# An encoder block on one core: the weights' sums of the feed-forward part spread over four stages

## The chip, the cores and the metric

The kernel runs on 1 core of one Trainium2 chip. The metric is the device time of one execution, in microseconds (us). The engines are TensorE (PE; its weight loads are PEld), VectorE (DVE), ScalarE (ACT), GpSimd (POOL) and SyncE (SP). Every DMA of this kernel is issued by SP, in one order; a DMA that has to wait for something holds up all that stand behind it on SP. A compile-time scheduler lays down the order of instructions on each engine; where the code calls `tc.keep_in_program_order`, the instructions so marked stay in the order of the code.

## The reference

One layer of a bidirectional encoder for two sequences of 512 tokens of width 1024, all in float32:

```python
mod = silu(c) @ w_ada + b_ada              # sh1, sc1, gt1, sh2, sc2, gt2
h = rmsnorm(x, g_attn) * (1 + sc1) + sh1
qa, ka, va, cq, ckv, kr, gla, glb = split(h @ w_in)
oa = windowed attention of qa, ka, va      # 8 heads, 2 key/value heads, +-128 tokens, sink
ob = dense attention from cq, ckv, kr      # 8 heads, low-rank q and kv
mix = sigmoid(gla) * (oa @ w_o_a) + sigmoid(glb) * (ob @ w_o_b)
x = x + gt1 * (mix @ w_out)
h2 = rmsnorm(x, g_ffn) * (1 + sc2) + sh2
u = dwconv3(h2 @ w_up)                     # to 2 x 2816 columns
x = x + gt2 * ((silu(ug) * ua) @ w_down)   # ua, ug: the two halves of u
```

## The kernel before

Matrix products are made of three matmuls each: a float32 operand is split into a high part (`hi`) and what is left (`lo`), and hi x hi, hi x lo and lo x hi are added (`mm3`, L80 to L82). The split of a weight is an operation of two halves: by POOL (`split_pool`, L70 and L73) or by ACT and DVE (`split_fast`, L76 and L77).

The program runs in stages. Up to about 230 us: modulation, norms, the projections of the attentions. From there to about 600 us: the two attentions. To about 693 us: the output weights of both mixers and the gates (`branches`), which leave `m_hi`, `m_lo`. To about 800 us: the product with `w_out` and the second norm (`project_half`). To about 1190 us: the first product of the feed-forward part and the convolution. The rest is the product with `w_down`.

**The weights' sums.** The first feed-forward product goes, for each of its 22 column chunks of 2 x 128, with seven block products instead of eight (Strassen's scheme in Winograd's form). For that, four sums of the four blocks of the chunk's weights are needed. They are made ahead, in the attention stage, by the generator `weight_sums` (L504 to L529), and are kept in DRAM, in `su_d`, which is read only in the feed-forward stage (`wraw<-su_d`, L764 by way of L969). The generator handles 44 half chunks. For each it loads a tile `wsum` of 128 x 4 x 256 (512 KB, L514), makes four sums on POOL in place (L522, L523, L525, L526), and stores the tile to `su_d` (L528). There are two buffers `wsum`. Loads, sums and stores are all pinned to the order of the code. Of each half, the load of the next half is put ahead of the sums, and the store behind them:

```python
for n, (c, cs) in enumerate(halves):
    t = ts[n]
    load(n + 1)
    pin(G.tensor_add(t[:, 3], t[:, 2], t[:, 3]))
```

A half takes three steps of the generator; the attention's loop advances it once a turn (`next(wsum, None)` at its end), and what is left is run through after the loop. The loop has 128 units of attention, 8 dense blocks (`PairB`) of 8 and 4 windowed blocks (`GroupA`) of 16.

**What stands around it.** Each turn of the loop also gives five matmuls of the generator `gates` (`psg`, L495) to PE, which fills the time between attention units. Every 24 of them end in a copy `go` by ACT (L499, two buffers) and a store of it (L500). The softmax (L531 to L540) scales its tile `p` on POOL (L539); PE then transposes `p` into `ppt` (L545). So POOL's sums and the `p` that PE waits for share one queue. The inputs of the windowed blocks are loaded as `lda` (L637), the outputs are stored as `o` (L614, L711), and the gates' weights are `wg_raw` (L480) and `wg`.

**Behind it.** In the branches the attention's output comes back as `o_raw` (2 MB each), and per pair of output chunks four tiles `wo_raw` (L804) are loaded and split by POOL into `wo`; PE's products are `psy`, 24 matmuls for each output chunk and sequence, 96 for a pair. `gt` is the load of the gates (L810). Behind the third pair of four the first half of `w_out` is loaded and split by POOL (`w_half(0)`, tiles `wraw` with seven buffers and `wt` with eight). `project_half(0)` makes the first 512 columns of the eight token tiles (`psx`, 24 matmuls each, over k = 0 to 7), adds x and stores (`x_d<-x`, L885; `x1_d` in the code). `w_half(1)` brings the second half of `w_out` (8 raw tiles, L762 to L764, split by ACT and DVE), and `project_half(1)` makes the other columns, the norm and the operands of the feed-forward part. There `tmp` gives small tiles; its kind `tmp_cc` (128 x 512) has six buffers.

## Time and profile before

| what | value |
|---|---|
| median of three runs | 1458.52 us (1457.64 to 1461.35) |
| the profiled execution | 1463.69 us |
| its span in the trace | 1461.9 us |
| PE busy | 1395.4 us, 95% of the span |
| PEld, weight loads beside PE | 1155.7 us, 79% |
| DVE, ACT, POOL busy | 64%, 46%, 42% |
| the chain that ended last | PE 78%, DVE 10%, DMA 5%, POOL 3%, ACT 2% |

The profile is of one execution. Its busy shares are means over stages with different limits, so the stretches have to be looked at one by one; the 5% of DMA and 3% of POOL in the chain lie where PE stood still for them. The granted clock of PE is a share of the higher of two levels (2.4 and 1.2 GHz).

### The profile page before, as it was taken

The page shows a single profiled execution, that of the slowest core. Times are in us where ns is not written, and L with a number is a line of the kernel's source. Part 1 is how long each engine was busy: PE and PEld are TensorE (multiplying, and loading weights), DVE is VectorE, ACT ScalarE, POOL GpSimd, SP SyncE. Part 2 cuts the span into 40 slices and gives each one's busy share as a digit, 9 for nine tenths or more (in the row PEclk, how much of TensorE's full clock was granted, in tenths as well). Part 3 has the DMA queues.
Part 4 walks back from the last instruction along what each step waited for, and adds up shares of the span by engine and source line. Part 5 has one row for each costly group of instructions (what it writes and reads, how often), then busy time and mean ns, then how long its engine had stood idle before and what let it go on. Part 6 is the DMA issues. An engine that isn't in the chain of part 4 may idle for free.

```text
span 1461.9 us, 21179 instructions
## 1 busy us (share of the span) xinstructions
PE 1395.4 (95%) x7184; PEld 1155.7 (79%) x7184; DVE 941.7 (64%) x1885; ACT 679.5 (46%) x1385; POOL 609.0 (42%) x702
## 2 busy tenths in 40 slices
PE   5888997999999899999998999999999999999998
PEld 4777776888878787787887888888888887888887
DVE  4788774666668786564369776666666668347433
ACT  3475223666666566332136765555555554212210
POOL 3175023676677787455003232222222235444430
PEclk9999999999999999999999999999999999999999
DMA  8565764666666667855432344444434447646522
GB/s 320 195 209 178 239 234 159 196 227 202 227 198 220 208 212 250 286 174 177 143 115 80 108 130 130 125 127 123 130 123 127 132 122 250 205 140 222 185 80 72
DMA packets 162620, 255.19 MB, mean 175 GB/s; under 512 B 21192, under 2 KB 86984, under 8 KB 159440
## 3 DMA queue, kind: packets, MB, share of 16 engines
q1 hardware_dynamic: 162512, 253.84, 53.2%
q8 instruction: 57, 0.93, 0.3%
q14 instruction: 51, 0.42, 0.1%
HBM read 186.67 MB, written 67.13 MB: 174 GB/s over the span
## 4 chain that ended last, share of the span: by engine, by line
PE 78%; DVE 10%; DMA 5%; POOL 3%; ACT 2%; issue 2%; SPq 0%; ACTq 0%; POOLq 0%; DVEq 0%
PE px L980 15%; PE psg L495 9%; PE py L980 8%; PE psd L80 5%; PE psd L81 5%; PE psd L82 5%; PE pz L980 4%; PE ppt L545 3%; PE ppo L608 2%; PE psx L82 2%; PE psx L81 2%; PE psx L80 2%; PE psz L80 1%; PE psz L82 1%; PE psz L81 1%
## 5 line engine op out<-in xcount | busy, mean ns | idle before, releaser
L959 POOL TENSOR_TENSOR wt<-wraw,wt 128x512 fp32r<-128x512 f32 x88 | 119.4, 1363 | 395.4 <-ACT wt L958 362.9
L980 PE MATMUL px<-t,wt 128*128 128x512 f32 x792 | 190.0, 389 | 1.7 <-ACT tmp_cc L985 1.7
L980 PEld LDWEIGHTS px<-t,wt 128*128 128x128 f32 x792 | 148.5, 188 | 33.1 <-ACT tmp_cc L985 2.4
L495 PE MATMUL psg<-h_hi,wg 128*128 128x512 f32 x512 | 172.1, 401 | 0.0
L77 DVE TENSOR_TENSOR wd<-wraw,wd 128x512 fp32r<-128x512 f32 x88 | 96.3, 1133 | 90.8 <-ACT wd L76 90.8
L80 PE MATMUL psd<-wd 128*128 128x512 f32 x352 | 137.0, 389 | 0.1
L82 PE MATMUL psd<-wd 128*128 128x512 f32 x352 | 136.9, 389 | 0.0
L81 PE MATMUL psd<-wd 128*128 128x512 f32 x352 | 136.9, 389 | 0.0
L76 ACT CAST wd<-wraw 128x512 fp32r<-128x512 f32 x88 | 50.8, 619 | 151.5 <-issue 112.7
L958 ACT CAST wt<-wraw 128x512 fp32r<-128x512 f32 x154 | 93.9, 619 | 39.7 <-POOL wt L959 26.5
L495 PEld LDWEIGHTS psg<-h_hi,wg 128*128 128x128 f32 x512 | 97.0, 192 | 18.7 <-POOL wg L73 0.8
L539 POOL TENSOR_SCALAR p<-p,l 128x512 f32<-128x512 f32 (+2 forms) x128 | 78.3, 615 | 63.7 <-DVE l L538 45.9
L495 PE MATMUL psg<-h_lo,wg 128*128 128x512 f32 x256 | 102.7, 401 | 0.0
L537 ACT ACTIVATE p<-pps,nm 128x512 f32<-128x512 f32 (+2 forms) x128 | 78.1, 610 | 39.2 <-DVE nm L534 31.3
L992 DVE SCALAR_TENSOR_TENSOR tmp_u<-tmp_cc,cw,tmp_u 128x511 f32<-128x511 f32 x66 | 57.2, 867 | 41.5 <-ACT tmp_u L991 41.4
L70 POOL TENSOR_SCALAR wd<-wraw 128x512 fp32r<-128x512 f32 x44 | 33.6, 764 | 112.5 <-PE psd L82 84.9
L80 PEld LDWEIGHTS psd<-wd 128*128 128x128 f32 x352 | 66.1, 188 | 14.3 <-issue 0.5
L82 PEld LDWEIGHTS psd<-wd 128*128 128x128 f32 x352 | 66.1, 188 | 13.8
L81 PEld LDWEIGHTS psd<-wd 128*128 128x128 f32 x352 | 66.1, 188 | 13.5
L534 DVE TENSOR_REDUCE nm<-pps 128x1 f32<-128x512 f32 (+2 forms) x128 | 74.7, 584 | 3.2 <-PE pps L82 1.5
L545 PE MATMUL ppt<-ident,p 128*128 128x128 f32 x416 | 66.9, 274 | 8.2 <-POOL p L539 8.2
L73 POOL TENSOR_TENSOR wd<-wraw,wd 128x512 fp32r<-128x512 f32 x44 | 73.1, 1661 | 3.7
(256 smaller groups left out, 3425.7 us busy)
## 6 DMA issues: line engine op xcount, KB each, us to landing
w_ada<-in_w_ada_dram SPq DMA_DIRECT2D x24, 1024.0 KB, 5.5
wsum<-in_w_up_dram SPq DMA_DIRECT2D x44, 512.0 KB, 3.9
su_d<-wsum SPq DMA_DIRECT2D x44, 512.0 KB, 3.6
wraw<-su_d SPq DMA_DIRECT2D x88, 256.0 KB, 3.1
wraw<-in_w_down_dram SPq DMA_DIRECT2D x88, 256.0 KB, 3.2
wraw<-in_w_up_dram SPq DMA_DIRECT2D x66, 256.0 KB, 2.7
g_d<-tmp_u SPq DMA_DIRECT2D x44, 256.0 KB, 2.4
wraw<-g_d SPq DMA_DIRECT2D x44, 256.0 KB, 3.5
```

The costliest lines, as they stand in the source:

```text
L77: V.tensor_sub(lo, raw, hi.bitcast(F32))
L80: PE.matmul(ps, lhsT=lh, rhs=rh, start=first, stop=False)
L81: PE.matmul(ps, lhsT=lh, rhs=rl, start=False, stop=False)
L82: PE.matmul(ps, lhsT=ll, rhs=rh, start=False, stop=last)
L495: PE.matmul(ps, lhsT=ws[n][:, wl, k, :], rhs=hl[b][:, k, :], start=k == 0 and i == 0, stop=k == KD - 1 and i == 2)
L534: V.tensor_reduce(nm, ps[:, :n], op=ALU.max, axis=AX.X, negate=True)
L537: A.activation(p[:, :n], ps[:, :n], AF.Exp, bias=nm, accum_out=l)
L539: G.tensor_scalar(out=p[:, :plen], in0=p[:, :plen], scalar1=l, scalar2=1.0, op0=ALU.mult, op1=ALU.mult)
L545: PE.transpose(pt[:, j * 128:(j + 1) * 128], p[:, j * 128:(j + 1) * 128], ident)
L958: A.copy(w[:, 0], raw)
L959: lo_eng.tensor_sub(w[:, 1], raw, w[:, 0].bitcast(F32))
L980: PE.matmul(ps[:, sl], lhsT=w[:, wl, i], rhs=h[:, hl, sl], start=not add and i == 0 and n == 0, stop=i == 3 and n == 2, skip_group_check=add)
```

## The change

`weight_sums` is now a function of its own that can be run in several places. It takes a maker of tiles, a width, a count and how many loads go ahead. All calls take their work from one list of 88 quarter chunks (128 columns each). Loads go `ahead` tiles before the sums, and the store of a tile is issued after the sums of the next tile. The calls:

- attention: 27 halves of 256 columns, three buffers, one load ahead plus the one at each tile; the loop advances it each turn up to turn 61, then each third turn; the rest is run through behind the loop
- branches: 6 halves, in tiles that share the `wt` buffers, three loads ahead, three steps after each call of `branches`
- `project_half(0)`: the last 22 quarters, in `tmp_cc` tiles, four loads ahead, nine steps (three quarters) after each token tile; the rest is run through behind it

Beside that, `go` has one buffer instead of two, and the raw tiles of the second half of `w_out` are asked for one after each token tile of `project_half(0)` but the first; the eighth is still asked for in `w_half(1)`, behind all quarters.

```diff
+    quarters = [(c, 128 * q) for c in ORDER for q in range(4)]
+    def weight_sums(tile, width, count, ahead):
+        pin = tc.keep_in_program_order
+        loaded = []
+        def load():
+            if len(loaded) < count and quarters:
+                c, c0 = quarters[0]
+                del quarters[:width // 128]
+                t, cs = tile(), slice(c0, c0 + width)
+                pin(SY.dma_start(t, w_up[c].rearrange("m q p n -> p (m q) n")[:, :, cs]))
+                loaded.append((t, su_d[c, :, :, cs]))
+        for _ in range(ahead):
+            load()
+        yield
+        yield
+        n, summed = 0, None
+        while n < len(loaded):
+            t, dst = loaded[n]
+            n += 1
+            load()
+            pin(G.tensor_add(t[:, 3], t[:, 2], t[:, 3]))
+            pin(G.tensor_sub(t[:, 2], t[:, 0], t[:, 2]))
+            yield
+            pin(G.tensor_sub(t[:, 0], t[:, 3], t[:, 0]))
+            pin(G.tensor_sub(t[:, 1], t[:, 1], t[:, 0]))
+            yield
+            if summed:
+                pin(SY.dma_start(*summed))
+            summed = (dst, t)
+            yield
+        if summed:
+            yield
+            yield
+            pin(SY.dma_start(*summed))
...
-                    go = gw.tile([128, S], F32, name="go", bufs=2)
+                    go = gw.tile([128, S], F32, name="go", bufs=1)
...
-        wsum = weight_sums()
+        wsum = weight_sums(lambda: gw.tile([128, 4, 256], F32, name="wsum", bufs=3), 256, 27, 1)
...
-            next(wsum, None)
+            if n < 62 or n % 3 == 2:
+                next(wsum, None)
...
-    def w_half(hf):
+    def w_raw(hf, k):
+        return wraw(w_out[k * 128:(k + 1) * 128, hf * HD:(hf + 1) * HD])
+    def w_half(hf, raws=()):
...
-            raw = wraw(w_out[k * 128:(k + 1) * 128, hf * HD:(hf + 1) * HD])
+            raw = raws[k] if k < len(raws) else w_raw(hf, k)
...
+        wsum = weight_sums(lambda: wp.tile([128, 4, 256], F32, name="wsum", tag="wt", bufs=8), 256, 6, 3)
...
                     branches(f + q, b, wo[q])
+                    for _ in range(3):
+                        next(wsum, None)
...
-        project_half(0, (0, 1), lambda b, i: None)
-        ws = w_half(1)
+        wsum = weight_sums(lambda: tmp("cc").rearrange("p (m n) -> p m n", m=4), 128, 4 * NP, 4)
+        raws = []
+        def sums(b, i):
+            for _ in range(9):
+                next(wsum, None)
+            if (b, i) > (0, 0):
+                raws.append(w_raw(1, len(raws)))
+        project_half(0, (0, 1), sums)
+        for _ in wsum:
+            pass
+        ws = w_half(1, raws)
```

How instructions stand at three places, before and after (a number behind a tile's name counts tiles; line numbers behind the inserted function are higher after).

SP in the windowed blocks, before: `su_d<-wsum` is the store of a summed tile, `wsum<-in_w_up_dram` the load of another.

```order
L514 DMA wsum_6826<-in_w_up_dram 128x4x256
L514 DMA wsum_6925<-in_w_up_dram 128x4x256
L500 DMA gate_d_62<-go_7017 128x512
L528 DMA su_d_67<-wsum_6826 512x1x256
L711 DMA o_d_63<-o_6915 128x512
L528 DMA su_d_67<-wsum_6925 512x1x256
L514 DMA wsum_7000<-in_w_up_dram 128x4x256
L514 DMA wsum_7093<-in_w_up_dram 128x4x256
L500 DMA gate_d_62<-go_7158 128x512
L528 DMA su_d_67<-wsum_7000 512x1x256
```

After, with the same names:

```order
L543 DMA gate_d_62<-go_6073 128x512
L492 DMA su_d_67<-wsum_5400 512x1x256
L523 DMA wg_raw_6784<-in_w_g_dram 128x1024
L473 DMA wsum_6192<-in_w_up_dram 128x4x256
L543 DMA gate_d_62<-go_6209 128x512
L725 DMA o_d_63<-o_6111 128x512
L543 DMA gate_d_62<-go_6380 128x512
L492 DMA su_d_67<-wsum_5664 512x1x256
L725 DMA o_d_63<-o_6351 128x512
L473 DMA wsum_6488<-in_w_up_dram 128x4x256
```

Between the store of one `wsum` tile and a later load there now stand a store of gates, an output or a weight load.

POOL in the branches, before: the splits of the first pair's last two `wo` tiles, and behind them those of the second pair.

```order
L70 TENSOR_SCALAR wo_7355<-wo_raw_7356 128x512
L73 TENSOR_TENSOR wo_7355<-wo_raw_7356,wo_7355 128x512
L70 TENSOR_SCALAR wo_7355<-wo_raw_7360 128x512
L73 TENSOR_TENSOR wo_7355<-wo_raw_7360,wo_7355 128x512
L70 TENSOR_SCALAR wo_7500<-wo_raw_7501 128x512
L70 TENSOR_SCALAR wo_7500<-wo_raw_7505 128x512
L73 TENSOR_TENSOR wo_7500<-wo_raw_7501,wo_7500 128x512
L73 TENSOR_TENSOR wo_7500<-wo_raw_7505,wo_7500 128x512
```

After, from behind the fourth split of the first pair and eight sums:

```order
L485 TENSOR_TENSOR wsum_7283<-wsum_7283 128x256
L486 TENSOR_TENSOR wsum_7283<-wsum_7283 128x256
L488 TENSOR_TENSOR wsum_7283<-wsum_7283 128x256
L489 TENSOR_TENSOR wsum_7283<-wsum_7283 128x256
L485 TENSOR_TENSOR wsum_7285<-wsum_7285 128x256
L486 TENSOR_TENSOR wsum_7285<-wsum_7285 128x256
L71 TENSOR_SCALAR wo_7409<-wo_raw_7410 128x512
L74 TENSOR_TENSOR wo_7409<-wo_raw_7410,wo_7409 128x512
L71 TENSOR_SCALAR wo_7409<-wo_raw_7414 128x512
L74 TENSOR_TENSOR wo_7409<-wo_raw_7414,wo_7409 128x512
L71 TENSOR_SCALAR wo_7418<-wo_raw_7419 128x512
L71 TENSOR_SCALAR wo_7418<-wo_raw_7423 128x512
```

Between the fourth split of the first pair and the second pair's `wo` there are 14 sums now, six of which stand here.

SP between the two halves of the projection, before: `x1_d` is the store of x, `wraw<-in_w_out_dram` the eighth raw tile of the second half of `w_out`, `tmp_u0` a load of the gates' gain.

```order
L885 DMA x1_d_65<-x1_0_8006 128x512 x2
L901 DMA tmp_u0_8309<-gt_d_66 128x512
L885 DMA x1_d_65<-x1_0_8006 128x512
L885 DMA x1_d_65<-x1_1_8007 128x512 x3
L764 DMA wraw_8304<-in_w_out_dram 128x512
L764 DMA wraw_8820<-in_w_up_dram 128x512
```

After, the last seven stores of sums, and what stands around and behind them:

```order
L492 DMA su_d_67<-tmp_cc_8143 512x1x128
L492 DMA su_d_67<-tmp_cc_8200 512x1x128
L473 DMA tmp_cc_8255<-in_w_up_dram 128x4x128
L492 DMA su_d_67<-tmp_cc_8150 512x1x128
L473 DMA tmp_cc_8262<-in_w_up_dram 128x4x128
L492 DMA su_d_67<-tmp_cc_8207 512x1x128
L906 DMA x1_d_65<-x1_1_7930 128x512
L492 DMA su_d_67<-tmp_cc_8248 512x1x128
L492 DMA su_d_67<-tmp_cc_8255 512x1x128
L498 DMA su_d_67<-tmp_cc_8262 512x1x128
L779 DMA wraw_8381<-in_w_out_dram 128x512
L922 DMA tmp_u0_8568<-gt_d_66 128x512
```

The eighth raw tile is now behind the store of the last quarter, `tmp_cc_8262`. The six loads of `w_up` behind it follow it as before.

PE at the start of the second half, before: `wt_8306` is the eighth tile of `w_out`'s second half and `psx_8312`, `psx_8357` the first two token tiles.

```order
L80 MATMUL psx_8312<-wt_8301,m_hi1_7344 128x512
L81 MATMUL psx_8312<-wt_8301,m_hi1_7344 128x512
L82 MATMUL psx_8312<-wt_8301,m_lo1_7345 128x512
L80 MATMUL psx_8312<-wt_8306,m_hi1_7344 128x512
L81 MATMUL psx_8312<-wt_8306,m_hi1_7344 128x512
L82 MATMUL psx_8312<-wt_8306,m_lo1_7345 128x512
L80 MATMUL psx_8357<-wt_8271,m_hi1_7344 128x512
L81 MATMUL psx_8357<-wt_8271,m_hi1_7344 128x512
```

After, where `wt_8383` is the eighth tile, `wt_8369` the seventh, and `psx_8389`, `psx_8434`, `psx_8479` are the first three token tiles:

```order
L81 MATMUL psx_8479<-wt_8369,m_hi1_7225 128x512
L82 MATMUL psx_8479<-wt_8369,m_hi1_7225 128x512
L81 MATMUL psx_8389<-wt_8383,m_hi1_7225 128x512
L81 MATMUL psx_8434<-wt_8383,m_hi1_7225 128x512
L83 MATMUL psx_8479<-wt_8369,m_lo1_7226 128x512
L82 MATMUL psx_8389<-wt_8383,m_hi1_7225 128x512
L83 MATMUL psx_8389<-wt_8383,m_lo1_7226 128x512
L82 MATMUL psx_8434<-wt_8383,m_hi1_7225 128x512
L83 MATMUL psx_8434<-wt_8383,m_lo1_7226 128x512
```

The products with the eighth tile now come behind those of three token tiles with the seven others: 21 + 21 + 11 matmuls.

## Rows read from the trace of the kernel before

**Rows 1.** Busy time by stretch, TensorE first; then clock, DMA share, GB/s.

```profile
240.00:420.00 180.00, 178.70 (x956) 148.88 (x955) 120.58 (x233) 114.99 (x245) 121.00 (x164) 1.00 0.62 204
420.00:440.00 20.00, 18.47 (x102) 15.14 (x101) 15.08 (x36) 13.07 (x31) 10.78 (x15) 1.00 0.71 231
480.00:520.00 40.00, 35.28 (x193) 29.51 (x191) 29.04 (x88) 23.19 (x61) 30.49 (x45) 0.96 0.70 222
575.00:590.00 15.00, 11.40 (x51) 9.12 (x50) 4.65 (x9) 7.91 (x17) 8.00 (x13) 0.89 0.58 181
590.00:620.00 30.00, 27.48 (x119) 21.81 (x118) 16.77 (x23) 9.97 (x15) 12.96 (x13) 1.00 0.91 306
780.00:800.00 20.00, 16.00 (x83) 13.84 (x82) 19.12 (x42) 11.55 (x30) 12.32 (x8) 0.83 0.37 116
```

**Rows 2.** TensorE's waits, 220 to 600 us: total, times, longest.

```profile
PE ppt L545 <- POOL p L539: 8.2, 5, 3.4
```

**Rows 3.** Chain of waits, 478 to 500 us: start, length, what.

```profile
486.28 3.37 DMA su_d<-wsum
...
489.66 5.93 DMA wsum<-in_w_up_dram
```

**Rows 4.** Chain of waits, 570 to 620 us.

```profile
571.54 1.15 PE psg L495 x5
...
575.86 4.81 DMA wsum<-in_w_up_dram
580.81 0.73 POOL wsum L522
581.61 0.72 POOL wsum L523
...
584.09 2.13 PE psg L495 x5
...
601.48 7.24 DMA wo_raw<-in_w_o_dram
```

**Rows 5.** Waits of SyncE's DMA queue, 230 to 601 us: total, times, longest.

```profile
SPq L528 <- POOL wsum L526: 94.4, 30, 7.6
SPq L514 <- DMA su_d<-wsum: 86.2, 36, 4.7
```

**Rows 6.** DMA issues, whole span: count, KB each, median us to landing.

```profile
su_d<-wsum SPq DMA_DIRECT2D x44, 512.0 KB, 3.6
...
wraw<-in_w_up_dram SPq DMA_DIRECT2D x66, 256.0 KB, 2.7
...
o_raw<-o_d SPq DMA_DIRECT2D x2, 2048.0 KB, 9.9
...
x_d<-x SPq DMA_DIRECT2D x8, 256.0 KB, 2.0
```

**Rows 7.** TensorE's timeline, 586 to 626 us: start, length, what, [idle before].

```profile
600.56 0.47 PE L80 MATMUL psy<-o,wo 128*128 128x512 f32 x1 [0.77 <-POOL wo L73]
```

**Rows 8.** SyncE's timeline, 684 to 830 us.

```profile
705.80 0.33 SPq L885 DMA_DIRECT2D x_d<-x  x1
...
733.78 0.33 SPq L764 DMA_DIRECT2D wraw<-in_w_out_dram  x1
```

**Rows 9.** VectorE's timeline, 725 to 752 us.

```profile
731.72 0.69 DVE L882 TENSOR_TENSOR tmp_u<-psx,tmp_u 128x512 f32<-128x512 f32 x1 [4.02 <-PE psx L82]
...
742.60 0.69 DVE L882 TENSOR_TENSOR tmp_u<-psx,tmp_u 128x512 f32<-128x512 f32 x1 [2.83 <-PE psx L82]
```

**Rows 10.** POOL's groups by line and form: busy us, mean ns | idle before.

```profile
L73 POOL TENSOR_TENSOR wt<-wraw,wt 128x512 fp32r<-128x512 f32 x8 | 10.3, 1290 | 0.7
```

**Rows 11.** Tile `wsum`, by line: duration ns min/median/max, first and last start.

```profile
L514 SPq DMA_DIRECT2D wsum<-in_w_up_dram x44: 368/379/938, 236.9 to 587.5; - x44
...
L528 SPq DMA_DIRECT2D su_d<-wsum x44: 518/519/857, 255.3 to 600.9; - x44
```

**Rows 12.** ScalarE's timeline, 728 to 745 us.

```profile
734.23 3.55 ACT L76 CAST wt<-wraw 128x512 fp32r<-128x512 f32 x6
```

More of the change, by code (lines that the diff above doesn't have):

```diff
@@ L34 @@
 NP = FF // 128
+ORDER = range(NP)
 EPS = 1e-6
@@ L497, in gates @@
                             yield
-                    go = gw.tile([128, S], F32, name="go", bufs=2)
+                    go = gw.tile([128, S], F32, name="go", bufs=1)
                     A.copy(go, ps)
                     SY.dma_start(gate_d[b, f, :, m], go)
-        def weight_sums():
-            pin = tc.keep_in_program_order
-            halves = [(c, slice(256 * q, 256 * (q + 1))) for c in range(NP) for q in range(2)]
-            ts = {}
-            def load(n):
-                if n < len(halves):
-                    c, cs = halves[n]
-                    ts[n] = gw.tile([128, 4, 256], F32, name="wsum", bufs=2)
-                    pin(SY.dma_start(ts[n], w_up[c].rearrange("m q p n -> p (m q) n")[:, :, cs]))
-            load(0)
-            yield
-            yield
-            for n, (c, cs) in enumerate(halves):
-                t = ts[n]
-                load(n + 1)
-                pin(G.tensor_add(t[:, 3], t[:, 2], t[:, 3]))
-                pin(G.tensor_sub(t[:, 2], t[:, 0], t[:, 2]))
-                yield
-                pin(G.tensor_sub(t[:, 0], t[:, 3], t[:, 0]))
-                pin(G.tensor_sub(t[:, 1], t[:, 1], t[:, 0]))
-                yield
-                pin(SY.dma_start(su_d[c, :, :, cs], t))
-                yield
         def softmax(ps, n, plen):
```

## The prediction

> **What bounds the kernel now.** I read the profile in this order: the busy time by stretch, to find where TensorE (PE) stands still; PE's waits there; the chain of waits through those stalls; and then, for the places that get new work, the waits of the DMA queue on SyncE (SP), the DMA landings and the timelines of SP and GpSimd (POOL). PE is the bound nearly everywhere, so a change gains only where PE is idle or runs at the lower clock level, and costs where it makes PE wait anew. In the dense attention, 240 to 420 us, PE is busy 178.70 of 180 us [rows 1]: nothing is to be had there. In the windowed attention there are two dents: 480 to 520 us (busy 35.28 of 40 us, so idle 4.72 us, granted clock 0.96) and 575 to 590 us (idle 3.60 us, clock 0.89) [rows 1]. PE waits there for `p` on POOL, 8.2 us in 5 waits, the longest 3.4 us [rows 2]. The chain says why: the store of one sum tile (3.37 us) must land before the load into the same of two buffers can go (5.93 us), POOL's next sum waits for that load, and `p`, which PE needs, stands behind this sum in POOL's order [rows 3]. The second dent is the same: a 4.81 us load, the sums, and only then PE's next matmuls [rows 4]. On SP the stores wait 94.4 us for the sums behind which they stand, and the loads 86.2 us in 36 waits for stores [rows 5].
>
> **Part 1, the sums in the attention (a gain).** 27 of 44 half tiles stay here; from step 62 of the loop on only every third step advances them, there are three buffers, and a store goes out one tile after its sums. The order shows it: in the last blocks a load is no longer next to the store it waits for, other DMAs stand between. So the waits of rows 2 to 4 should go. What they are worth: the idle time 4.72 + 3.60 = 8.3 us, and the slow matmuls after each stall. Five `psg` matmuls take 1.15 us before the second stall and 2.13 us after it [rows 4], 1.9 times as long: the lower of the two clock levels. Taking the granted clock of the two stretches, (1 - 0.96) x 40 + (1 - 0.89) x 15 = 3.3 us are lost so. Together 11.6 us. The 1.5 us of 420 to 440 us [rows 1] come from a late `lda` load that stood behind a store of sums; half of it, 0.7 us, I count as won. I take **-12.3 us**, between -8 (some stalls come back in the next late thing, the DVE and ACT steps of the softmax) and -14. `go` has one buffer instead of two: its copies are 24 matmuls apart and a store lands in 3 or 4 us, so I cost it at nothing, except at the end of the stage (part 2).
>
> **Part 2, six half tiles in the output branches.** PE lost 30 - 27.48 = 2.5 us at 590 to 620 us [rows 1], to output weights `wo` that were late (a 7.24 us load in the chain [rows 4]). Now the first four splits of `wo` come right after the last `p`, but the third and fourth raw tile load behind the 2 MB `o_raw`, which takes 9.9 us to land [rows 6]; then 14 sums stand in POOL's queue ahead of the `wo` of the second pair. 14 x 0.80 us (from the start of a sum to that of the next [rows 4]) = 11.2 us. The fourth split ends near 609, some 2 us earlier than now, so the sums are through at 620 if their loads are there, at 625 if these queue behind `o_raw`, the gate stores and `gt`; the next split needs 1.9 us more. PE wants it 96 matmuls after the first `psy` at 600.56 [rows 7], at some 623. That is 0 to 4 us of new wait, against 1 to 2 us that the earlier splits save. The trace shows no such crowding of loads, so the bounds are -2 and +4; I take **+2 us**, nearer the upper since DMA is already at 0.91 of its time there [rows 1].
>
> **Part 3, the last 22 quarters in the first projection (a cost).** Before, POOL had nothing to do here and SP little. Now 88 sums of 128 columns, 22 loads and 22 stores of 256 KB stand there, and one thing stands behind all of them: the eighth raw tile of the second half's output weights. Seven are loaded early, as before. The eighth was loaded at 733.78 us, between two stores of x [rows 8]; in the new order it is behind the store of quarter 21. So the question is when SP gets there.
> When PE wants it: the first tile of the second half ended at 742.60 us, two tiles of 24 matmuls after 731.72 [rows 9]: 10.88 / 48 = 0.227 us each, 5.4 us a tile, so the second half begins at 737.2 us. PE's new order puts 53 matmuls ahead of the eighth tile (7 pieces of two products and 11 matmuls of a third): 737.2 + 53 x 0.227 = 749.2 us.
> When POOL can be done: the first loads follow the first store of x, 705.80 us [rows 8], and land at about 705.8 + 0.4 + 2.7 (a 256 KB load of `w_up` [rows 6]) = 708.9. A sum of 256 columns takes 0.73 us [rows 4], a POOL operation of the same kind on 512 columns 1.29 us [rows 10], so one of 128 about 0.73 - 0.56 / 2 = 0.45, and with the gap that sums show now (0.80 from start to start of 0.73 us [rows 4]) 0.53 us. Four make 2.1 us, 22 quarters 46.6 us: not before 755.5 us, were every load there in time.
> When SP can be done: with six buffers, load n waits for store n - 6. In the new order this store stands directly ahead of the load, or one DMA ahead, for 11 of the 16 loads after the first six, so each is a full round trip. A store of sums landed in 3.6 us (512 KB), a store of x in 2.0 us (256 KB) [rows 6]; by SP's own waits, 86.2 / 36 = 2.4 us [rows 5] plus 0.5 us of its issue, it was 2.9 us. Here each store follows a load of its own size within half a microsecond, so I take 3.2 us: 11 x 3.2 = 35.2 us. The first store goes at 708.9 + 2.1 = 711.0 or so. The rest of the issuing: 16 loads x 0.38, 8 other DMAs x 0.33, 5 stores outside the round trips x 0.52 = 11.3 us (issue times as in [rows 8] for 0.33; 0.38 and 0.52 are medians of a load and a store of sums [rows 11]). 757.5 us; the last load lands (2.7) and is summed (2.1), its store is issued (0.5): 762.8 us. The weights land 2.7 us later and are cast by ACT in 0.6 us (six take 3.55 us [rows 12]): 766.1 us. PE stands from 749.2 to 766.1: **+17 us**. Lower bound: POOL alone sets the pace, 755.5 + 0.5 + 2.7 + 0.6 - 749.2 = 10 us, or 8 if a sum takes no gap. Upper bound: 3.6 us a round trip and 3.9 us for the weights, as for other loads beside much traffic, 23 us.
> On page "DMA: Bandwidth & Descriptors" (section "Anatomy of one DMA") the Trainium skill gives a DMA a fixed cost of about 2.0 us plus bytes at 436 GB/s, which it says is mostly the receipt of the last byte and doesn't shrink with size; this speaks against splitting half tiles into quarters, for the round trips then double. By it a 256 KB store would land in 2.6 us, an estimate, and the chain would end some 6 us earlier, near POOL's own bound.
> After the stall PE runs at the lower clock level for a while: 2.13 instead of 1.15 us for five matmuls and as much again for the next [rows 4], **+2 us** (1 to 3). What follows, the last norms on DVE with 4.0 us of idle PE at 780 to 800 us [rows 1], depends on the second half's products alone and only moves; the DVE order there changes in a few places, which I cost at nothing (-2 to +2).
>
> **The sum.** -12.3 + 2 + 17 + 2 = +8.7 us. The profiled execution took 1463.7 us (span 1461.9 us), 5 us above the median of the three plain runs, 1458.5 us; on the median the sum gives 1467 us.
>
> **Rivals.** (a) *POOL paces it.* If stores land as fast as those of x (2.0 us), SP is never late and the wait is POOL's 10 us: -12.3 + 2 + 10 + 2 = +1.7, 1460 us. For it: the quick x stores with 0.33 us issues in this very stage [rows 8]; against it: their rows are 2 KB long, the quarters' 512 bytes, and loads run beside them. The Trainium skill's formula above would land near this rival. (b) *Faster after all.* The wait for the eighth tile is 4 us or less, because the quarters start earlier or a sum of 128 columns takes 0.40 us: -12.3 + 0 + 4 + 1 = -7, 1451 us. It decides where 22 quarters take less than 41 us from the first landing. For it: POOL is otherwise empty there; against it: a quarter would have to take 1.85 us, less than the scaling of [rows 4, 10] gives with its gaps. (c) *Worse.* Loads and stores slow each other to 4 us a round trip, as the 5.93 us load did [rows 3], and the branches pay 4 us: -12.3 + 4 + 28 + 2 = +22, 1480 us. (d) *The attention stalls stay* (the stores still hold SP): -4 + 2 + 17 + 2 = +17, 1475 us; the new order speaks against it.
>
> **How the numbers follow.** Forecast 0.50, (a) 0.22, (b) 0.12, (c) 0.09, (d) 0.07. A measurement here can tell 0.3%, 4.4 us, from no change. The forecast's spread (1462 to 1473) lies almost all above 1462.9, (c) and (d) above, (a) mostly within, (b) below: slower 0.64, same 0.22, faster 0.14. The range leaves out (b)'s lower part and (c)'s upper: 1453 to 1477.
>
> **What would show it.** In the new profile: no wait of `ppt` for `p` above 1 us at 440 to 590 us, and the attention's end some 12 us earlier; a PE wait of 10 to 25 us in `psx` some 12 us into the second half, released by ACT's cast of `wt` and behind it by the load of `w_out`; SP rows of loads of `tmp_cc` waiting for stores of `su_d` some ten times, 2 to 3 us each. It is wrong if `psx` doesn't wait (then b), if the `p` waits remain (d), or if the branch stage loses over 5 us.

## The result

The changed kernel is slower: 1478.22 us median of four runs (1476.15 to 1482.98) against 1458.64 us (1457.64 to 1461.35). The ratio is 1.0136, with a 95% interval of 1.0108 to 1.0164, or 16 to 24 us. The forecast was 1467 us with a range of 1453 to 1477 us, so the sign was right and the time lies just above the range; the loss of 19.6 us was sized at 8.7 us.

Four points in TensorE's own order show where the time went: the first and last `psg` (the gates, which fill the attention), the first `psy` (branches), the first `psx` (projection) and the first `px` with `t` (feed-forward part). They stand in the views by tile; columns: duration in ns (min/median/max), first and last start in us. Before:

```profile
L495 PE MATMUL psg<-h_hi,wg x512: 387/393/775, 216.6 to 599.4; 128*128 128x512 f32 x171
...
L80 PE MATMUL psy<-o,wo x128: 387/389/501, 600.6 to 692.8; 128*128 128x512 f32 x128
...
L80 PE MATMUL psx<-wt,m_hi x128: 389/389/500, 693.4 to 785.4; 128*128 128x512 f32 x128
...
L980 PE MATMUL px<-t,wt x792: 387/389/496, 818.4 to 1217.4; 128*128 128x512 f32 x198
```

After:

```profile
L538 PE MATMUL psg<-h_hi,wg x512: 387/393/776, 213.0 to 580.4; 128*128 128x512 f32 x171
...
L81 PE MATMUL psy<-o,wo x128: 389/389/765, 586.8 to 680.8; 128*128 128x512 f32 x128
...
L81 PE MATMUL psx<-wt,m_hi x128: 387/389/792, 681.5 to 798.7; 128*128 128x512 f32 x128
...
L1013 PE MATMUL px<-t,wt x792: 387/389/499, 831.3 to 1230.0; 128*128 128x512 f32 x198
```

| stretch | before | after | difference | forecast |
|---|---|---|---|---|
| attention, first to last `psg` | 382.8 us | 367.4 us | -15.4 | -12.3 |
| last `psg` to first `psy` | 1.2 | 6.4 | +5.2 | 0 |
| branches, first `psy` to first `psx` | 92.8 | 94.7 | +1.9 | +2 |
| projection, first `psx` to first `px` with `t` | 125.0 | 149.8 | +24.8 | +19 |
| sum | 601.8 | 618.3 | +16.5 | +8.7 |

Ahead of the first `psg`, where nothing was changed, the profiled execution after was 3.6 us shorter; that is why the two spans, 1461.9 and 1474.4 us, differ by 12.5 only. In the traces of all runs below this point lies between 212.1 and 218.3 us, so one stretch of one trace is good to some us. TensorE's waits after, whole span (total us, times, longest):

```profile
PE psx L81 <- ACT wt L77: 17.3, 1, 17.3
...
PE psy L81 <- issue: 6.0, 1, 6.0
...
PE pst L887 <- DVE x L913: 3.4, 2, 2.2
PE psy L81 <- POOL wo L71: 3.0, 1, 3.0
...
PE psy L83 <- POOL wo L74: 1.1, 1, 1.1
...
PE ppt L559 <- POOL p L553: 0.2, 1, 0.2
```

The wait of [rows 2], 8.2 us for `p`, is down to 0.2 us. In its place stand the forecast wait of `psx` for the eighth weight tile (17.3 us) and one that was not forecast, 6.0 us of `psy` at the end of the attention. The stretches of after that answer to [rows 1] (us, then busy time of PE, PEld, DVE, ACT, POOL, then granted clock, DMA share, GB/s):

```profile
480.00:520.00 40.00, 39.64 (x225) 33.31 (x224) 34.83 (x107) 27.88 (x73) 21.02 (x32) 1.00 0.34 112
580.00:590.00 10.00, 3.99 (x12) 2.88 (x11) 4.00 (x5) 4.86 (x10) 4.19 (x4) 0.66 0.97 334
590.00:620.00 30.00, 30.00 (x134) 24.82 (x133) 18.30 (x23) 9.67 (x11) 26.17 (x29) 1.00 0.89 293
650.00:660.00 10.00, 5.97 (x23) 4.33 (x22) 2.70 (x4) 1.06 (x1) 9.75 (x11) 0.91 0.62 214
737.00:754.50 17.50, 0.24 (x2) 0.03 (x1) 0.05 (x1) 0.62 (x1) 10.70 (x24) 0.59 0.91 266
754.50:760.00 5.50, 5.50 (x13) 4.34 (x14) 2.75 (x6) 1.46 (x3) 0.00 (x0) 0.50 0.95 331
785.00:815.00 30.00, 21.95 (x120) 18.99 (x119) 27.18 (x67) 18.51 (x47) 12.15 (x8) 0.89 0.30 97
```

The windowed attention is full (39.64 of 40 us where it was 35.28). TensorE then stands at 580 to 587 us and at 737 to 754 us, each time with DMA at more than 0.9 of its time, and comes back at the lower clock level (0.50 of full speed after the second). The branches run full from 590 to 620 us and stand still once, 4.1 us for `wo` between 650 and 660 us. 785 to 815 us is the tail of the projection, where VectorE is busy 27.18 of 30 us; it holds 8.05 us of idle TensorE where [rows 1] had 4.00.

### The profile page after: what moved, and what is told of

Same layout as the page of the kernel before. It is cut to its first block, busy times and chain, and to the rows that moved or that the text cites. A ratio compares the mean times of both kernels' runs of the same rounds, so it can differ in the third digit from the quotient of the medians.

```text
span 1474.4 us, 21271 instructions
## 1 busy us (share of the span) xinstructions
PE 1395.1 (95%) x7184; PEld 1156.8 (78%) x7184; DVE 944.2 (64%) x1885; ACT 679.4 (46%) x1385; POOL 624.4 (42%) x746
## 4 chain that ended last, share of the span: by engine, by line
PE 76%; DVE 10%; POOL 5%; DMA 4%; ACT 2%; issue 2%; SPq 0%; ACTq 0%; POOLq 0%; DVEq 0%
PE px L1013 15%; PE psg L538 11%; PE py L1013 8%; PE psd L81 5%; PE psd L83 5%; PE psd L82 5%; PE pz L1013 4%; PE ppt L559 3%; PE ppo L622 2%; PE psz L81 1%; PE psz L83 1%; PE psz L82 1%; DMA gt<-gate_d 1%; PE pps L693 1%; PE ppo L717 1%
## 5 line engine op out<-in xcount | busy, mean ns | idle before, releaser
L78 DVE TENSOR_TENSOR wd<-wraw,wd 128x512 fp32r<-128x512 f32 x88 | 97.3, 1144 | 91.4 <-ACT wd L77 91.3
L82 PEld LDWEIGHTS psd<-wd 128*128 128x128 f32 x352 | 66.1, 188 | 13.7
L1024 ACT ACTIVATE tmp_u<-tmp_cc,cw 128x512 f32<-128x512 f32 x66 | 53.6, 812 | 36.0 <-DMA g_d<-tmp_u 28.7
```

What stands on the lines that cost most here:

```text
L78: V.tensor_sub(lo, raw, hi.bitcast(F32))
L82: PE.matmul(ps, lhsT=lh, rhs=rl, start=False, stop=False)
```

## The experiments

The runs were made on several chips, on which the kernel before took 1459 to 1466 us in the median; all are compared by their ratio to it. The last four columns are the stretches of the table above, read in the same way from each trace.

| run | ratio, interval | attention | gap | branches | projection |
|---|---|---|---|---|---|
| before | 1 | 382.8 | 1.2 | 92.8 | 125.0 |
| the change | 1.0136 (1.0108 to 1.0164) | 367.4 | 6.4 | 94.7 | 149.8 |
| e1_raw8_first | 1.0084 (1.0055 to 1.0112) | 369.5 | 6.8 | 97.3 | 143.9 |
| e2_go_first | 1.0128 (1.0089 to 1.0167) | 370.2 | 5.9 | 96.2 | 150.0 |
| e3_both | 1.0081 (1.0052 to 1.0110) | 367.7 | 6.4 | 97.6 | 142.5 |
| e4_no_quarters | 0.9981 (0.9962 to 1.0000) | 369.2 | 6.6 | 98.1 | 126.8 |
| e6_two_sums | 1.0078 (1.0049 to 1.0107) | 369.5 | 6.5 | 96.5 | 145.5 |
| g1_attention_only | 0.9945 (0.9925 to 0.9965) | 369.9 | 7.0 | 94.4 | 126.4 |
| g3_go_freed | 1.0159 (1.0136 to 1.0183) | 367.5 | 10.0 | 99.9 | 146.7 |
| g5_all_in_attention | 1.0011 (0.9997 to 1.0024) | 374.8 | 9.5 | 93.0 | 126.2 |
| g6_ten_quarters | 0.9993 (0.9980 to 1.0006) | 369.2 | 9.8 | 98.8 | 126.7 |
| h1_go_in_wg_raw | 1.0139 (1.0115 to 1.0163) | 368.1 | 1.1 | 105.3 | 146.5 |
| h2_ten_quarters_go | 0.9969 (0.9954 to 0.9983) | 368.0 | 1.1 | 105.4 | 126.3 |
| h3_no_branch_sums | 0.9905 (0.9886 to 0.9924) | 371.4 | 1.1 | 92.4 | 126.3 |
| h4_all_in_attention_go | 0.9970 (0.9955 to 0.9985) | 373.6 | 1.1 | 97.6 | 126.0 |

### The projection: what stands behind the quarters

**e1_raw8_first** takes the eighth raw tile out from behind the quarters.

```diff
-        r = wp.tile([128, 512], F32, name="wraw", bufs=7)
+        r = wp.tile([128, 512], F32, name="wraw", bufs=8)
...
-            if (b, i) > (0, 0):
+            if True:
                 raws.append(w_raw(1, len(raws)))
```

> The changed kernel, but all eight raw tiles of the second half of w_out are asked for during the first projection half, ahead of the quarters (one buffer more for raw tiles); the quarters are all there. Theory A: what the projection lost is the wait for the eighth tile, 17.3 us in the trace of the changed kernel, and what follows from it (lower clock and work of VectorE bunched behind it, the other 7.6 us between this point and the first feed-forward matmul with t): 1478.2 - 24.9 = 1453 us, 1450 to 1457, and no wait of psx above 2 us. Rival B: the quarters load DMA and POOL so that something else is late in their place (the x tiles, the w_up tiles): 1465 to 1476.

Theory A fell and rival B held. The wait of `psx` is gone, but the projection still takes 143.9 us, 19 more than before. TensorE now waits for VectorE (TensorE's waits of e1, 680 to 840 us; total us, times, longest):

```profile
PE pst L887 <- DVE x L913: 17.4, 4, 5.0
```

Behind that ScalarE waits for a store (ScalarE's timeline of e1; start, length, what, [idle before <- releaser]):

```profile
759.94 0.63 ACT L907 ACTIVATE tmp_u<-tmp_u 128x512 f32<-128x512 f32 x1 [19.64 <-DMA x_d<-tmp_u]
```

And SP issues this store just behind that of the last quarter (SP's timeline of e1):

```profile
755.38 0.51 SPq L498 DMA_DIRECT2D su_d<-tmp_cc  x1
755.95 0.62 SPq L906 DMA_DIRECT2D x_d<-tmp_u  x1
```

Each token tile of the second half is left in one of two `tmp_u1` buffers and stored from there; ScalarE's squares of the norm use the same two. While the first store stands in SP's queue behind the quarters, the second tile's norm can't be made, and VectorE can't go on. So the eighth tile was only the first of several things of the second half that stand behind the quarters; freed alone, it uncovers the next.

**e4_no_quarters** is the bound: no quarters at all.

```diff
-        wsum = weight_sums(lambda: tmp("cc").rearrange("p (m n) -> p m n", m=4), 128, 4 * NP, 4)
+        wsum = weight_sums(lambda: tmp("cc").rearrange("p (m n) -> p m n", m=4), 128, 0, 4)
...
-                yield split_w(wraw(su_d[c, :, q]), eng)
+                yield split_w(wraw(su_d[c, :, q] if c < 16 else w_up[c, q // 2, q % 2]), eng)
```

> The changed kernel without the 22 quarters (work left out: the sums of the last 5.5 chunks are not made; the feed-forward part reads plain blocks of w_up in place of all sums of the last six chunks, so its loads and matmuls stay). By theory A the quarters cost nothing beside the eighth tile: the same as with the eighth tile first, 1453 us, within 3. By rival B they cost more: 4 us or more below that kernel.

The projection is back to 126.8 us; rival B held here too. The quarters cost 149.8 - 126.8 = 23 us; the ratio falls from 1.0136 to 0.9981.

**e6_two_sums** asks what sets the end of the quarters: POOL's pace or the round trips on SP.

```diff
-            pin(G.tensor_sub(t[:, 2], t[:, 0], t[:, 2]))
+            if width == 256:
+                pin(G.tensor_sub(t[:, 2], t[:, 0], t[:, 2]))
...
-            pin(G.tensor_sub(t[:, 1], t[:, 1], t[:, 0]))
+            if width == 256:
+                pin(G.tensor_sub(t[:, 1], t[:, 1], t[:, 0]))
```

> The changed kernel with two instead of four sums for each of the 22 quarters (work left out: the second and the fourth sum of these quarters; loads and stores stay as they are). Theory P: POOL's pace sets the end of the quarters (88 sums, 50 us from the first to the last, next to no idle time): with 44 sums of 0.54 us the quarters end some 12 to 20 us earlier, the wait of psx for the eighth tile falls from 17.3 to below 6 us, and the projection takes some 130 to 135 us instead of 149.8. Theory S (the prediction's): the round trips on SP set it: the wait stays above 12 us.

By its number theory S held: `psx` still waits 13.7 us, above the 12 us named, and the projection takes 145.5 us (TensorE's waits of e6, 230 to 840 us):

```profile
PE psx L81 <- ACT wt L77: 13.7, 1, 13.7
```

But this doesn't show that the round trips set the end in the change itself. With half of POOL's work gone, the time from the start of the first sum to that of the last falls from 50.1 to 46.0 us (view of the tile `tmp_cc` by line, after; the last line is who waited for the tile, in all and how often):

```profile
L485 POOL TENSOR_TENSOR tmp_cc<-tmp_cc x22: 453/460/910, 699.7 to 748.2; 128x128 f32<-128x128 f32 x22
...
L489 POOL TENSOR_TENSOR tmp_cc<-tmp_cc x22: 455/462/795, 701.3 to 749.8; 128x128 f32<-128x128 f32 x22
...
POOL tmp_cc L485: 35.7, 5
```

The same view of e6:

```profile
L485 POOL TENSOR_TENSOR tmp_cc<-tmp_cc x22: 452/459/972, 703.1 to 748.6; 128x128 f32<-128x128 f32 x22
L489 POOL TENSOR_TENSOR tmp_cc<-tmp_cc x22: 452/462/857, 703.6 to 749.1; 128x128 f32<-128x128 f32 x22
...
POOL tmp_cc L485: 57.7, 17
```

Of these waits the first, 34.6 us in after and 34.7 us in e6, lies ahead of the first sum. So between its first and last sum POOL waited for loads 1.1 us in the change and 23.0 us in e6: in the change POOL itself sets the pace, in e6 the round trips do. SP shows the same from its side. Its waits of after, 690 to 752 us (total us, times, longest):

```profile
SPq L492 <- POOL tmp_cc L485: 12.1, 7, 3.1
SPq L473 <- DMA su_d<-tmp_cc: 10.1, 11, 2.9
```

And of e6:

```profile
SPq L473 <- DMA su_d<-tmp_cc: 16.6, 14, 3.2
...
SPq L494 <- POOL tmp_cc L485: 2.7, 3, 1.9
```

So the two limits are some 4 us apart: POOL's sums come last in the change, and with half of those sums gone the round trips still take 46 us.

**g6_ten_quarters** moves 12 quarters back to the attention, so that the rest ends before the second half begins (it also has the edits of e1 and g3).

```diff
-        wsum = weight_sums(lambda: gw.tile([128, 4, 256], F32, name="wsum", bufs=3), 256, 27, 1)
+        wsum = weight_sums(lambda: gw.tile([128, 4, 256], F32, name="wsum", bufs=3), 256, 33, 1)
...
-            if n < 62 or n % 3 == 2:
+            if n < 87 or n % 3 == 2:
...
```

> 33 half tiles in the attention, 6 in the branches, the last 10 quarters in the first projection half; all eight raw tiles asked for ahead of the quarters, and the last go copy freed. Theory A2: the quarters cost only because POOL is through with them some 25 us after the second half has begun, and everything that SP issues for the second half (eighth raw tile, stores of x from two tmp_u buffers, a gain) stands behind them. Ten quarters take 10 x 2.2 = 22 us from the first landing, so they end before the second half begins (44 us after the first psx): the projection takes 125 us from its first matmul to the first px with t, as before. 0.993 of the kernel before. Rival B2: any quarters there cost by their traffic: 0.997 or more.

For the projection theory A2 held: 126.7 us, as with no quarters at all (126.8). Twelve cost nothing either (h3: 126.3). The ratio came out at 0.9993, not 0.993: the rest was lost ahead of the projection, as follows.

### The end of the attention and the branches

The 6.0 us of `psy` are put down to "issue", which names no cause. ScalarE's timeline of after does:

```profile
585.12 1.14 ACT L77 CAST o<-o_raw 128x512 fp32r<-128x512 f32 x2 [9.06 <-DMA o_raw<-o_d]
586.16 0.58 ACT L542 COPY go<-psg 128x512 f32<-128x512 f32 x1
```

The last `go` copy ends at 586.74, `psy` begins at 586.84. The copy reads the last `psg` out of PSUM, and by the code the pool of `psy` takes the place of the attention's pools, that of `psg` among them. In e2 (copy to 588.60, `psy` from 588.71) and h1 (581.94 and 582.04) `psy` follows this copy by 0.1 us as well. In the kernel before this copy stood ahead of the casts; now it is behind two of them, and these wait for the 2 MB load of `o_raw` [rows 6].

**e2_go_first** puts the copy back ahead of the casts, **e3_both** adds the edit of e1.

```diff
+        copied_go = []
...
-                    A.copy(go, ps)
+                    copied_go.append(A.copy(go, ps))
...
-                split_fast(o[0][:, q, :], o[1][:, q, :], raws[b][:, q, :])
+                if b:
+                    with tc.issue_after(copied_go[-1].ins):
+                        split_fast(o[0][:, q, :], o[1][:, q, :], raws[b][:, q, :])
+                else:
+                    split_fast(o[0][:, q, :], o[1][:, q, :], raws[b][:, q, :])
```

> The changed kernel, but ScalarE makes the last copies of go ahead of the casts of the second o_raw, as the kernel before did; go keeps its one buffer. Theory C: the 6.0 us in which TensorE stands still at the end of the attention (580.8 to 586.8) come from the last go copy, which stands behind two casts that wait for the 2 MB load of o_raw; the copy frees the PSUM bank that psy needs. 1478.2 - 6.0 - 2.0 (slow matmuls behind the stall) = 1470 us, 1468 to 1472. Rival D: psy waits for output weights there, whose loads stand behind o_raw: 1476 to 1479.

> Both edits of the two kernels above together. By theories A and C: 1478.2 - 24.9 - 8.0 = 1445 us, 1441 to 1450, and 0.992 of the kernel before. By B and D: above 1462. If the early start of the branches only runs into late output weights, the second edit gives nothing back here and it is 1453.

Nothing was won (e3 is no better than e1), and theory C fell as it stood: the copy is first in line now and waits all the same, for the store of the copy before it. ScalarE's timeline of e2:

```profile
588.02 0.58 ACT L544 COPY go<-psg 128x512 f32<-128x512 f32 x1 [9.64 <-DMA gate_d<-go]
```

This is the single `go` buffer, whose last store was issued behind the load of `o_raw`. No run gives `go` its second buffer back.

**g3_go_freed** gives the last copy a tile of `p` in place of `go`, beside the edit of e2; **h1_go_in_wg_raw** gives it a tile of `wg_raw`.

```diff
-                    go = gw.tile([128, S], F32, name="go", bufs=1)
+                    if n == 2 * KD - 1 and b:
+                        go = wk.tile([128, 513], F32, name="p", bufs=4)[:, :S]
+                    else:
+                        go = gw.tile([128, S], F32, name="go", bufs=1)
...
```

> The changed kernel, but the last go copy goes ahead of the casts of the second o_raw and into a free buffer of p, so it needs neither the load of o_raw nor the store of the copy before it. Theory C2: two things hold this copy, one behind the other: its place behind the casts and, where that is mended alone, the single go buffer, whose last store lands late beside the 2 MB load of o_raw (with the order mended ScalarE waited 9.6 us for this store). With both gone the 6.0 us at the end of the attention and the slow matmuls behind go: 8 us, 1470 us or 1.008 of the kernel before. Rival D: psy then waits for wo instead and nothing is won: 1.013.

> The changed kernel, but the last go copy goes ahead of the casts of the second o_raw and into a tile of wg_raw that is free by then. In the run with a tile of p the loads of wo_raw, whose memory lies where p was, stood behind the store of this tile; wg_raw's memory is not reused by wo_raw. Theory C3: the single go buffer and the place of its last copy cost 6.0 us of standing and about 2 us of slow matmuls: psy starts within 1.5 us of the last psg, 1470.5 us, 1.0085 of the kernel before. Rival G: the end of the attention is bound by DMA (o_raw with 2 MB, stores, weights at once), so that whatever is freed, psy starts some 6 to 10 us after the last psg: 1.012 to 1.016.

In g3 the next thing took the place: SP issued the first loads of `wo_raw` at 585.81 us (572.57 in the change), behind loads of `wraw` that waited for a gate store, and this store of 256 KB, issued behind `o_raw`, took 8.46 us (chain of waits of g3):

```profile
576.30 8.46 DMA gate_d<-go
...
586.23 3.77 DMA wo_raw<-in_w_o_dram
```

In h1 the end of the attention is mended: `psy` begins 1.1 us after the last `psg`. Yet the ratio stays at 1.0139, since the branches take 105.3 us. TensorE's timeline of h1:

```profile
582.04 0.47 PE L81 MATMUL psy<-o,wo 128*128 128x512 f32 x1 [0.72 <-POOL wo L74]
...
611.33 0.80 PE L81 MATMUL psy<-o,wo 128*128 128x512 f32 x1 [4.34 <-POOL wo L71]
```

POOL's timeline of h1:

```profile
605.76 1.14 POOL L486 TENSOR_TENSOR wsum<-wsum 128x256 f32<-128x256 f32 x1
610.65 0.62 POOL L71 TENSOR_SCALAR wo<-wo_raw 128x512 fp32r<-128x512 f32 x1 [3.75 <-DMA wo_raw<-in_w_o_dram]
```

TensorE waits for the second pair's `wo`. On POOL it stands behind 14 sums, the last at 605.76, and its raw tile comes late even then, since on SP it stands behind loads and stores of sums (SP's timeline of h1):

```profile
604.84 0.52 SPq L492 DMA_DIRECT2D su_d<-wsum  x1
605.42 2.61 SPq L831 DMA_DIRECT2D wo_raw<-in_w_o_dram  x3
```

In the change, by contrast, TensorE waited for no `wo` of the second pair at all: the 6 us of standing ahead of the branches gave it time. So the sums in the branches are not as cheap as +1.9 us. The sum of gap and branches shows it: 94.0 us before; 101.4 with the gap and without sums (g1); 106.4 and 106.5 with sums and without the gap (h1, h2); 101.1 to 104.7 with both (the change, e1 to e4 and e6, of which the change's trace is the lowest); 93.5 with neither (h3). The last cell is not sharp: h4, also without both but with 44 half tiles in the attention, has 98.7 us, and `psy` waited 4.0 us for a late `wo` of the first pair there.

**g1_attention_only** leaves out the branch sums as well as the quarters.

```diff
-        wsum = weight_sums(lambda: wp.tile([128, 4, 256], F32, name="wsum", tag="wt", bufs=8), 256, 6, 3)
+        wsum = weight_sums(lambda: wp.tile([128, 4, 256], F32, name="wsum", tag="wt", bufs=8), 256, 0, 3)
...
-        wsum = weight_sums(lambda: tmp("cc").rearrange("p (m n) -> p m n", m=4), 128, 4 * NP, 4)
+        wsum = weight_sums(lambda: tmp("cc").rearrange("p (m n) -> p m n", m=4), 128, 0, 4)
...
```

> The changed kernel without the sums in the branches and without the quarters (work left out: the sums of the last 8.5 chunks are not made; the feed-forward part reads plain blocks of w_up in place of all sums of the last nine chunks). The difference to the kernel without quarters (0.998 of before) is what the six half tiles in the branches cost. If they cost the 3 us by which that stage grew: 0.996. If nothing: 0.998.

0.9945 against 0.9981: with the gap in place, the six half tiles cost 5 us by the ratios, 3.7 us in the branches of the two traces.

**h2_ten_quarters_go** is g6 with the copy in `wg_raw`.

> 33 half tiles in the attention, 6 in the branches, 10 quarters, raw tiles first, with this place for the last go copy. With it in p this was 0.999 of the kernel before, and psy started 9.8 us after the last psg. Theory C3: 0.9935 (1449 us on 1458.6). Rival G: 0.998 to 1.0.

0.9969 lies between the two: the gap is gone, and the branches take 105.4 us, as in h1.

### What the attention's part gives alone

**g5_all_in_attention** keeps all 44 half tiles in the attention, with a step each turn, three buffers and the late store, and the last copy in `p`; **h4_all_in_attention_go** is the same with the copy in `wg_raw`.

```diff
-        wsum = weight_sums(lambda: gw.tile([128, 4, 256], F32, name="wsum", bufs=3), 256, 27, 1)
+        wsum = weight_sums(lambda: gw.tile([128, 4, 256], F32, name="wsum", bufs=3), 256, 2 * NP, 1)
...
-            if n < 62 or n % 3 == 2:
-                next(wsum, None)
+            next(wsum, None)
...
```

> All 44 half tiles in the attention again, one step in each turn as in the kernel before, but with three buffers and the store one tile behind the sums; with the last go copy freed. No sums in the branches or the projection. Theory E: the buffers and the late store alone take away the stalls of the attention: 13 us off, nothing given back, 0.991 of the kernel before (1445 us on 1458.6). Rival F: it is the thinning of the sums in the windowed blocks that does it; with all 44 the stalls come back: 0.996 to 1.0.

> All 44 half tiles in the attention, three buffers, store one tile behind, the last go copy in wg_raw. In the run with p the attention took 374.8 us from the first to the last psg (382.8 before, some 369 where the sums are thinned), and psy came 9.5 us later. Theory E/F between them: the buffers and the late store win 8 us, the thinning 5 to 6 more. With the end freed (C3): 0.995. By G: 1.0.

Both theories hold in part. Third buffer and late store alone win 8 to 9 us of the attention (374.8 and 373.6 us against 382.8); thinning the sums in the windowed blocks brings some 5 more (367 to 370). In g5 the gap (9.5 us) took the gain back; in h4 it didn't, the branches took 4.8 us more than before, and 0.9970 remained.

**h3_no_branch_sums** puts together what the runs left standing: 38 half tiles in the attention, none in the branches, 12 quarters in the projection, eight raw buffers, the last copy in `wg_raw`.

> 38 half tiles in the attention (each turn up to turn 108, then each third), none in the branches, 12 quarters in the first projection half, raw tiles first, the last go copy in wg_raw. The sums in the branches cost 4 to 5 us (0.9981 against 0.9945); twelve quarters take 26 us and end about when the second half begins. If the attention still has its gain of 13 us: 0.991. If thicker sums in the windowed blocks bring the stalls back: 0.994 to 0.997.

Its expectation of 0.991 held: 0.9905 (0.9886 to 0.9924), about 14 us faster than the kernel before and 34 us faster than the change on 1458.6. Its stretches for comparison with those of after:

```profile
480.00:520.00 40.00, 39.10 (x227) 33.31 (x226) 33.56 (x102) 27.67 (x73) 33.83 (x51) 1.00 0.73 233
580.00:590.00 10.00, 9.28 (x41) 7.40 (x41) 1.42 (x3) 1.17 (x2) 5.65 (x6) 1.00 0.91 280
590.00:620.00 30.00, 29.29 (x130) 23.90 (x129) 19.51 (x27) 13.43 (x19) 11.07 (x10) 1.00 0.84 281
740.00:800.00 60.00, 54.79 (x301) 47.41 (x300) 53.25 (x135) 38.10 (x89) 12.33 (x8) 0.94 0.19 62
```

## Why the prediction was wrong

**Part 1, the attention: right.** The `p` waits went, and the gain was 15.4 us in the profiled run, 11 to 15 us in the others with thinned sums, for a term of 12.3.

**Part 1, one `go` buffer: the step that failed first.** It was costed "at nothing, except at the end of the stage (part 2)", and part 2 then had no term for it. The reason given, that copies are 24 matmuls apart and "a store lands in 3 or 4 us", fails at the one place that matters: there a store issued behind `o_raw` took 8.46 us (g3). The trace of the kernel before held the sign of it. Its store at 595.2 us, just behind `o_raw`, took 11.2 us to land, without harm, since the last copy had the second buffer (view of the tile `go`, 594 to 597 us):

```profile
L500 SPq DMA_DIRECT2D gate_d<-go x1: 542/542/542, 595.2 to 595.2; - x1
...
DMA to landing us min/median/max: 11.2/11.2/11.2
```

In the change the copy's new place behind two casts had the same effect; it can be read in ScalarE's order, while the prediction drew on those of SP, POOL and PE. The gap is 5.2 us longer, and the granted clock of 580 to 590 us was 0.66 on the mean.

**Part 2, the branches: right by chance.** +2 was forecast for a late `wo` of the second pair, and +1.9 came, but not from there: from 600 to 640 us `psy` waited for nothing. The 4.1 us at 650 to 660 us belong to the fourth pair, and g1, without sums in the branches, waits 3.3 us in that stretch too. The first seven `psy` behind the gap took 3.3 us, from 0.42 to 0.77 each, where seven take 1.6 us later on, at 0.23 each; these 1.7 us are most of the +1.9 (chain of waits of after; the second line is the first matmul at full pace):

```profile
586.84 0.77 PE psy L81
...
590.16 0.23 PE psy L82
```

In the five other traces with the gap and the same sums (e1 to e4, e6) the branches grew by 3.4 to 5.3 us. Without the gap, the same sums cost 105.3 - 92.4 = 13 us against h3 and 105.3 - 97.6 = 8 us against h4, which both also differ from h1 in the number of tiles in the attention. The upper bound of +4 was too low: the term counted POOL's queue and not that the second pair's raw weights stand behind the sums' loads and stores on SP as well.

**Part 3, the wait for the eighth tile: right in place and size, by luck in its mechanism.** 17.3 us for a term of 17. The prediction had the round trips on SP set the end: 11 of them, 3.2 us each. SP did wait for stores 11 times, but for 10.1 us in all, and POOL's sums came last, with 1.1 us of waits among 88 sums. That is the mechanism of rival (a), though not for its reason, stores of 2.0 us; and its price of 10 us was too low by 7.3 us: the first sum started 18.2 us behind the first `psx` for 15.5 assumed; the sums took 49.4 us for 46.6, since twelve of them took 0.79 to 0.91 us and not 0.46; the waits add 1.1 us. Together these are 6.6 us. The round trips are the next limit, 4 us behind (e6). The lower bound of 8 us for sums without a gap doesn't follow from its own price: 88 x 0.45 = 39.6 us would end 7 us earlier than 46.6, at a wait of 3 us.

A store of a quarter landed in 3.3 us in the median, for 3.2 assumed. The estimate of 2.6 us by the Trainium skill, page "DMA: Bandwidth & Descriptors", section "Anatomy of one DMA", is below that; the section speaks of DMAs that GpSimd issues, while all here are issued by SyncE, and DMA was at 0.88 of its time from 700 to 720 us.

**Part 3, the tail: the second step that failed.** The restart was sized +2 us and the tail behind it at nothing; together they measured 24.8 - 17.3 = 7.5. The lower clock took 0.50 x 5.5 = 2.75 us at 754.5 to 760 us, near its term. The sentence that the tail "depends on the second half's products alone and only moves" was wrong: the wait let three token tiles end close together, so VectorE, which bounds the tail, had stood idle with TensorE and then had their norms to make one behind the other. In the trace this is 8.05 us of idle TensorE at 785 to 815 us for 4.00 [rows 1]. That VectorE's late work costs these 4 us is read from the two timelines; no run took it away alone.

So the sum of +8.7 missed 5 us in the gap and 5.5 us in the restart and the tail, 3 us of which the larger gain in the attention gave back. In the plain runs the difference was 19.6 us (16 to 24), in the profiled executions 12.5: that of the kernel before, 1463.69 us, lay 5.1 us above its median, and that of the change 2.1 us below. The +16.5 of the four stretches therefore shows where the time went, and not its size to a few us.

## What to carry to other kernels

When a batch of work is put on a shared DMA queue, ask not only which transfer stands right behind it, but list everything of the next stage that does; freeing the first one uncovered the next here, and moving the batch's end ahead of the next stage made it free. Whether all of the next stage's transfers could have been issued ahead of the batch, or on another engine's queue, no run tried. When two limits lie close together, ask of each which one the engine really waited for: a run that halves one of them shows where the other lies, and not which one was ahead. Where a buffer is given up as unneeded, price it at the most crowded place of the program, not by its median. Two stalls in a row can cover each other, so a cost measured beside another stall is no cost of its own.

## What the runs showed of the hardware

A store of 256 KB, issued just behind a load of 2 MB, took 8.46 us to land in g3 and 11.2 us in the kernel before, against a median of 2.8 us for the stores of gates in the changed kernel's trace. POOL's sums of 128 columns took 0.46 us, but 0.79 to 0.91 us for eight of them from 721.5 to 729 us; VectorE was busy 8.73 of the 10 us from 720 on, mostly with splits that read two tiles from SBUF. The sum at 719.72 us, beside an operation of VectorE that reads one of its two inputs from PSUM, took 0.46 us. The Trainium skill, page "Advanced Engine Details and Errata", section "GPSIMD Details", says that POOL shares a read and a write interface with VectorE and conflicts with its instructions that have two SBUF inputs; the trace agrees, though no run was made on that.
